# A decoder trunk on one core: the S5 input matrices are split and written ahead of the S5 preparation, and the first unit's products go by weight rows

## The chip, the cores and the metric

The kernel runs on 1 core of one Trainium2 chip. The metric is device time in microseconds (us) of one execution; the median of three is given. Times inside an execution are microseconds from the start of its span. The engines are TensorE (PE; its weight loads are PEld), VectorE (DVE), ScalarE (ACT), GpSimd (POOL) and SyncE (SP, which here only issues DMAs). ACT and POOL issue DMAs too.

## The reference, cut to what matters

One layer, 256 positions, 2048 channels, all float32. The normalised input is projected by one wide matrix; three branches of 1024 channels (gated MLP, S5, stick-breaking attention) are gated, projected and added; an MLP of 8192 follows.

```python
h = rmsnorm(x, norm1_g[l])
proj = h @ w_in[l]
...
bb_re = k_re[..., None] * b_re - k_im[..., None] * b_im
bu_re = jnp.einsum('blgh,gph->blgp', u, bb_re)
...
_, _, s_re, s_im = lax.associative_scan(combine, (a_re, a_im, bu_re, bu_im), axis=1)
y = (jnp.einsum('blgp,ghp->blgh', s_re, c_re.astype(f32))
     - jnp.einsum('blgp,ghp->blgh', s_im, c_im.astype(f32)))
...
g = jax.nn.gelu(y)
out = g * jax.nn.sigmoid(g @ w_glu.astype(f32) + b_glu.astype(f32))
```

The S5 input matrices are `b_re` and `b_im`. The attention masks its scores, takes a softplus, sums it along the keys by a triangular matmul and exponentiates; the masked form is what POOL computes below.

## The kernel before, in words

**Weights by units.** All weights are read once, in 512 KB units of 256 rows by 512 columns (or the same bytes in a wider form). For each unit SP loads `raw` (L195; 4 buffers), ACT rounds it to `hi` (L214) and DVE subtracts `lo = raw - hi`; every DVE operation has line 86, that of the helper which meters it. TensorE multiplies hi by the split activations' hi and lo, and lo by their hi: three products in the place of one float32 product. `whi` and `wlo` hold 4 units each; `begin_unit(u)` asks for the conversion of unit u+3, so ACT and DVE work some units ahead and ACT mostly waits until TensorE gives a `hi` buffer back.

**Order.** PE, DVE, ACT and SP run in the order in which the program writes their instructions (`MANUAL`). POOL is not in that list: the framework's scheduler sets POOL's order by its own estimate of when each instruction is ready, and every engine then waits in its order at run time. The plan of units is: s5 (units 0 to 15), q0 (16 to 23), k0 (24 to 31), v0 (32 to 39), q1 (40 to 47), k1, v1, the two halves of vg and u (to 95), gates and branches (to 223), and the S5 branch's GLU from unit 224.

**Side work by credit.** Everything beside the units is a generator in the list `tasks`: the norm's sums (`rows`), the S5 preparation (`s5p`), the split of the S5 input matrices (`s5b`), the splits of S5's input (`su0`, `su1`), the S5 recurrence (`s5`), attention (`att0`, `att1`). After each unit `pump()` adds 2560 ns less what DVE's instructions since the last pump cost by the rule in `Metered` (65 + 1.042 ns per element of a row, or 0.52 in three cheap forms; 180 in place of 65 up to 128 elements); the credit is capped at two units. It then goes through the list from the front; each task runs until it yields BAR (it wants the next unit) or the credit is used up. `spawn` puts a task in front, or behind all others with `front=False`.

**Around the change.** In unit 7 `s5p` and then `s5b` are put at the back. `s5b` (L511 to L525) loads `br` (512 KB, from ACT's queue, L515), waits two units, rounds it to `bh` on ACT (L520), subtracts `bl` on DVE, waits one more, and POOL writes both to DRAM (`bd`, L524 and L525); it does this for two halves. `s5p` has only small DVE operations, two Sin on ACT (L586, L587), and no BAR between L589 and its end. `s5_go` waits until `s5p`, `s5b`, `su0` and `su1` are gone and three units more, then `s5_run` starts: POOL reads `bd` and the split input `ud` back in blocks (`bs`, L658; `su`, L659), DVE builds the first table (`tt`, `cs`), TensorE multiplies (`pb`, L672), and so on for 16 chunks. `do_glu` (L1066) first drains whatever is left of `s5`, down to the split of its result `gs`.

The norm's row factors take the path: `r_s` on DVE, its power on POOL (`r_r`, L385), `diag` on DVE, `prow` on TensorE (L500), `rbc` on ACT (L502); each step one unit after the last. The result of the first s5 group is multiplied by `rbc` on DVE into `s5x`, which gives its PSUM banks back to q0's products (unit 16). In attention's first pair of heads, `pz` on TensorE (L845), `za` on ACT (L852), its mask on POOL (L854), Abs, Exp and Ln on ACT (`le`, L859 to L861), `sp` on DVE and `pc` on TensorE (L871) follow each other from unit 40 to unit 45.

Of the kernel before, what the change touches and what calls it, by code (L numbers as in the profile page):

```python
# [17 lines left out]
P = 128  # L18
# [73 lines left out]
def hybrid_trunk(  # L92
# [22 lines left out]
    V, S, G, PE = Metered(nc.vector), nc.scalar, nc.gpsimd, nc.tensor  # L115
# [14 lines left out]
    def a4(shape, dt, name):  # L130
        return acts.tile(shape, dt, tag="a4", name=name)
# [68 lines left out]
    def conv_to(n, parts=1):  # L200
        while nconv[0] <= min(n, len(units) - 1):
            u = nconv[0]
            dma_to(u)
            raw = raws[u]
            raws[u] = None
            if u >= len(units) - 4:
                hi, lo = (a4([P, 2, 512], F32R, f"{n_}{u}") for n_ in ("hi", "lo"))
            else:
                hi = whi.tile([P, 2, 512], F32R, tag="hi", name=f"hi{u}")
                lo = wlo.tile([P, 2, 512], F32R, tag="lo", name=f"lo{u}")  # L210
            w = 2 // parts
            for j in range(parts):
                k = slice(j * w, j * w + w)
                S.copy(hi[:, k, :], raw[:, k, :])  # L214
                V.tensor_sub(lo[:, k, :], raw[:, k, :], hi[:, k, :].bitcast(F32))
            loaded[u] = (hi, lo)
            nconv[0] += 1
# [26 lines left out]
    def spawn(name, gen, front=True):  # L244
        tasks.insert(0 if front else len(tasks), (name, gen))
# [5 lines left out]
    def flush():  # L251
        due = [f for n, f in late if n <= slot[0]]
        late[:] = [e for e in late if e[0] > slot[0]]
        for f in due:
            f()
# [4 lines left out]
    def begin_unit(u, lead):  # L260
        dma_to(u + 5)
        conv_to(u + lead)
        flush()
        return loaded.pop(u)

    def end_unit():
        pump()
        slot[0] += 1

    def two_banks(name):  # L270
        return ps_mm.tile([P, 2, 512], F32, tag="mm", name=name)
# [34 lines left out]
    def run_T(us, src, evac, lead=3, mid=None, delay=1):  # L306

        pt = two_banks(f"mm{us[0]}")
        ps = [pt[:, b, :].rearrange("p (e t) -> p e t", e=2) for b in range(2)]
        nk = len(us)  # L310
        for i, u in enumerate(us):
            hi, lo = begin_unit(u, lead)
            for nb in range(4):
                po = ps[nb // 2][:, nb % 2, :]
                for k in range(2):
                    kt = 2 * i + k
                    wh = hi[:, k, nb * P:(nb + 1) * P]
                    PE.matmul(po, lhsT=wh, rhs=src.hi(kt), start=kt == 0 and nb % 2 == 0, stop=False)  # L318
                    PE.matmul(po, lhsT=wh, rhs=src.lo(kt), start=False, stop=False)  # L319
                if nb == 1 and mid is not None:  # L320
                    mid(i)
            for nb in range(4):
                po = ps[nb // 2][:, nb % 2, :]
                for k in range(2):
                    kt = 2 * i + k
                    PE.matmul(po, lhsT=lo[:, k, nb * P:(nb + 1) * P], rhs=src.hi(kt), start=False,  # L326
                              stop=kt == 2 * nk - 1 and nb % 2 == 1)
            if i == nk - 1:
                for b in range(2):
                    late.append((slot[0] + delay, lambda b=b: evac(b, ps[b])))  # L330
                flush()
            end_unit()
# [96 lines left out]
    def load_x(c):  # L429
        S.dma_start(xt[c], x[:, c * 512:(c + 1) * 512].rearrange("(a p) c -> p a c", p=P))  # L430
# [49 lines left out]
    def x_half(i):  # L480
        c, half = divmod(i, 2)
        split_scaled([xf[c][:, 2 * half + j, :] for j in range(2)], xs, 2 * i, C_G1)

    def norm1_sums():
        for c in range(4):
            for tt in range(NT):
                sumsq(xt[c][:, tt, :], ss1[:, tt, c:c + 1], xt[c][:, tt, :])
            yield BAR
        yield from norm1_rows()
# [21 lines left out]
    def s5_split_b():  # L511

        for i in range(2):
            br = a4([P, 4, 2 * P], F32, f"br{i}")
            S.dma_start(br, s5_b[:, 4 * i:4 * i + 4])  # L515
            yield BAR
            yield BAR
            hi = a4([P, 4, 2 * P], F32R, f"bh{i}")
            lo = a4([P, 4, 2 * P], F32R, f"bl{i}")
            S.copy(hi, br)  # L520
            V.tensor_sub(lo, br, hi.bitcast(F32))
            yield 1135
            yield BAR
            G.dma_start(bd[:, 4 * i:4 * i + 4, 0, :], hi)  # L524
            G.dma_start(bd[:, 4 * i:4 * i + 4, 1, :], lo)  # L525

    def s5_split_u(i):
        hi = a4([P, 4, T], F32R, f"uh{i}")
        lo = a4([P, 4, T], F32R, f"ul{i}")
        S.copy(hi, s5x[i])  # L530
        V.tensor_sub(lo, s5x[i], hi.bitcast(F32))
        yield 1135
        yield BAR
        G.dma_start(ud[:, 4 * i:4 * i + 4, 0, :], hi)
        G.dma_start(ud[:, 4 * i:4 * i + 4, 1, :], lo)
# [431 lines left out]
    def do_proj(kind, i, us):  # L967
        dsts = {"s5": s5x, "q": qT, "k": kT, "u": uT}[kind]

        def ev(b, ps):  # L970
            if dsts[i] is None:
                dsts[i] = a4([P, 4, T], F32, f"{kind}{i}")
            dst = dsts[i]
            o = dst[:, 2 * b:2 * b + 2, :]
            V.tensor_mul(o, ps if kind == "s5" else wide_sum(ps, f"w{kind}{i}_{b}"), rb)
            if kind == "u":
                def act():
                    S.activation(o, o, AF.Gelu_apprx_tanh)
                    if i == 1 and b == 1:
                        gm["u"] = True  # L980

                later(1, act)
            if kind == "s5" and b == 1:
                spawn(f"su{i}", s5_split_u(i))
                if i == 1:
                    spawn("s5", s5_go(), front=False)

        if kind == "s5":
            run_T(us, xs, ev)
        else:  # L990
            for j, u in enumerate(us):
                run_W([(u, lambda ps, j=j: ev(j, ps))], xs)
# [57 lines left out]
    def do_branch(n, d, us):  # L1050
        if n != 1:
            drain({2: "att1", 0: "gmlp"}[n])

        def ev(tt, ps):
            if n == 2:
                merged[d] = gate[n, d]
            g = gate[n, d][:, tt, :]
            m = merged[d][:, tt, :]
            V.tensor_mul(g, g, ps)
            if n != 2:  # L1060
                V.tensor_add(m, m, g)
            if n == 1 and tt == 1:
                spawn(f"mt{d}", merged_T(d))

        run_N(us, {2: yc, 0: ya, 1: yb}[n], ev)
# [90 lines left out]
    for kind, arg, us in plan:  # L1156
        if kind == "s5" and arg == 0:
            x_half(0)
            conv_to(0, parts=2)

            def ev0(b, ps):
                V.tensor_mul(s5x[0][:, 2 * b:2 * b + 2, :], ps, rb)
                if b == 1:
                    spawn("su0", s5_split_u(0))

            def mid0(i):
                if i == 0:
                    x_half(1)
                elif i in (1, 3, 5):
                    x_half(i + 1)  # L1170
                    conv_to(i + 1)
                    x_half(i + 2)
                conv_to(max(i + 1, {4: 6, 5: 7, 6: 8, 7: 10}.get(i, 0)))
                if i in (2, 3, 4, 5):
                    load_x(i - 2)
                if i == 6:
                    spawn("rows", norm1_sums())
                if i == 7:
                    spawn("s5p", s5_prep(), front=False)
                    spawn("s5b", s5_split_b(), front=False)  # L1180

            run_T(us, xs, ev0, lead=0, mid=mid0, delay=8)
        elif kind in ("s5", "q", "k", "u"):
            do_proj(kind, arg, us)
        elif kind in ("v", "vg"):
            do_nat(kind, arg, us)
        elif kind.startswith("gate"):
            do_gate(int(kind[4]), arg, us)
        elif kind.startswith("br"):
            do_branch(int(kind[2]), arg, us)  # L1190
        elif kind == "glu":
            do_glu(arg, us)
        elif kind == "out":
            do_out(arg, us)
        elif kind == "m1":
            do_m1(*arg, us)
        else:
            do_m2(*arg, us)
# [74 lines left out]
```

## Time and profile before

| what | value |
|---|---|
| median of 3 runs | 1553.64 us (1553.34 to 1557.04) |
| profiled execution, its own time | 1557.89 us |
| its span, first to last instruction | 1556.2 us |
| granted TensorE clock, mean | 0.993 of full |
| busy: PE, DVE, ACT, POOL | 1532.5, 1097.4, 763.1, 67.6 us |

Busy time is the sum of an engine's instructions. "Idle before, and its releaser" in a timeline row says how long the engine stood before the instruction and what ended that. A view of waits sums the same by pair. A clock of 1.00 is 2.4 GHz, 0.50 is 1.2 GHz; in a stretch with both the mean stands.

### The profile page before, as it was taken

What the parts mean: (1) busy time and instruction counts of PE and PEld (TensorE: products, weight loads), DVE (VectorE), ACT (ScalarE), POOL (GpSimd) and SP (SyncE); (2) the same over time, 40 slices, a digit from 0 to 9 for tenths busy, and PEclk for the clock granted to TensorE, in tenths of its full rate; (3) what the DMA queues carried; (4) which work ended last, traced back from release to release, by engine and by line L of the source; (5) the groups of instructions that cost most, each with busy time, mean ns of one, the idle gap of its engine ahead of it and who ended that gap; (6) DMA issues with size and microseconds to landing.
All of it is one profiled execution on the core that took longest, in us unless ns stands there. A gap on an engine that the chain in (4) does not pass through costs nothing.

```text
span 1556.2 us, 20753 instructions
## 1 busy us (share of the span) xinstructions
PE 1532.5 (98%) x7900; PEld 1307.7 (84%) x7900; DVE 1097.4 (71%) x1454; ACT 763.1 (49%) x947; POOL 67.6 (4%) x126
## 2 busy tenths in 40 slices
PE   9998999999999999999999999999999999999997
PEld 9986888888888888888888888888888888888886
DVE  6894798999999999967655665556545655556554
ACT  7445658554555554555445443344443443344442
POOL 0101111000101100000000000000000000000000
PEclk9998999999999999999999999999999999999998
DMA  8866566666766766646665555555555555555653
GB/s 328 259 209 201 151 206 192 206 182 200 229 199 210 217 203 198 204 159 201 196 223 183 189 187 197 191 190 190 189 192 197 182 191 198 191 190 190 216 192 106
DMA packets 97411, 308.67 MB, mean 198 GB/s; under 512 B 11296, under 2 KB 22560, under 8 KB 97312
## 3 DMA queue, kind: packets, MB, share of 16 engines
q1 hardware_dynamic: 79200, 285.25, 56.0%
q0 software_dynamic: 11904, 10.49, 3.3%
q10 hardware_dynamic: 6208, 11.61, 2.3%
q8 instruction: 62, 1.02, 0.3%
q14 instruction: 37, 0.30, 0.1%
HBM read 301.02 MB, written 6.29 MB: 197 GB/s over the span
## 4 chain that ended last, share of the span: by engine, by line
PE 89%; issue 5%; DVE 2%; ACT 1%; DMA 1%; POOL 0%; SPq 0%; POOLq 0%; DVEq 0%; ACTq 0%
PE mm L349 19%; PE mm L350 19%; PE mm L352 19%; PE mm L289 18%; PE mm L293 9%; PE mm L319 1%; PE mm L318 1%; PE mm L326 1%; PE py L770 1%; DVE lo L86 1%; DMA bd<-bh 0%; ACT hi L214 0%; PE pb L672 0%; DMA raw<-in_w_in 0%; DMA raw<-in_w_m 0%
## 5 line engine op out<-in xcount | busy, mean ns | idle before, releaser
L86 DVE TENSOR_TENSOR lo<-raw,hi 128x1024 fp32r<-128x1024 f32 (+1 forms) x537 | 652.8, 1220 | 389.2 <-ACT hi L214 373.7
L214 ACT CAST hi<-raw 128x1024 fp32r<-128x1024 f32 (+1 forms) x537 | 561.4, 1049 | 623.5 <-PE mm L350 374.3
L289 PE MATMUL mm<-xz,hi 128*128 128x512 f32 x1024 | 256.5, 392 | 0.0
L289 PEld LDWEIGHTS mm<-xz,hi 128*128 128x128 f32 x1024 | 184.5, 189 | 33.0
L349 PE MATMUL mm<-hi,xs 128*128 128x512 f32 x512 | 200.9, 392 | 0.0
L350 PE MATMUL mm<-hi,xs 128*128 128x512 f32 x512 | 199.6, 390 | 0.0
L350 PE MATMUL mm<-hi,ff 128*128 128x512 f32 x480 | 186.9, 389 | 0.0
L349 PE MATMUL mm<-hi,ff 128*128 128x512 f32 x480 | 186.9, 389 | 0.0
L293 PEld LDWEIGHTS mm<-xz,lo 128*128 128x128 f32 x1024 | 139.8, 191 | 9.9
L293 PE MATMUL mm<-xz,lo 128*128 128x256 f32 x1024 | 142.8, 283 | 0.0
L352 PE MATMUL mm<-lo,xs 128*128 128x512 f32 x512 | 137.0, 390 | 0.0
L352 PE MATMUL mm<-lo,ff 128*128 128x512 f32 x480 | 128.3, 389 | 0.0
L349 PEld LDWEIGHTS mm<-hi,xs 128*128 128x128 f32 x512 | 96.2, 188 | 21.9 <-ACT bu L679 2.1
L352 PEld LDWEIGHTS mm<-lo,xs 128*128 128x128 f32 x512 | 96.2, 188 | 20.1
L350 PEld LDWEIGHTS mm<-hi,xs 128*128 128x128 f32 x512 | 96.3, 188 | 19.2
L352 PEld LDWEIGHTS mm<-lo,ff 128*128 128x128 f32 x480 | 90.1, 188 | 18.7
L349 PEld LDWEIGHTS mm<-hi,ff 128*128 128x128 f32 x480 | 90.1, 188 | 18.7
L350 PEld LDWEIGHTS mm<-hi,ff 128*128 128x128 f32 x480 | 90.2, 188 | 18.4
L289 PE MATMUL mm<-xs,hi 128*128 128x512 f32 x384 | 97.7, 397 | 0.0
L289 PEld LDWEIGHTS mm<-xs,hi 128*128 128x128 f32 x384 | 69.8, 191 | 12.6
L86 DVE TENSOR_TENSOR rt<-bu,cs 128x1024 f32<-128x1024 f32 x64 | 76.3, 1218 | 0.2
L293 PEld LDWEIGHTS mm<-xs,lo 128*128 128x128 f32 x384 | 52.4, 190 | 3.8
(252 smaller groups left out, 1689.3 us busy)
## 6 DMA issues: line engine op xcount, KB each, us to landing
raw<-in_w_m SPq DMA_DIRECT2D x256, 512.0 KB, 4.3
raw<-in_w_in SPq DMA_DIRECT2D x143, 512.0 KB, 4.2
raw<-in_w_wide SPq DMA_DIRECT2D x48, 512.0 KB, 4.2
raw<-in_w_br SPq DMA_DIRECT2D x48, 512.0 KB, 4.2
raw<-in_w_out SPq DMA_DIRECT2D x32, 512.0 KB, 4.0
x<-in_x ACTq DMA_DIRECT2D x8, 512.0 KB, 5.9
raw<-in_w_glu SPq DMA_DIRECT2D x8, 512.0 KB, 4.2
su<-ud POOLq DMA_DIRECT2D x48, 64.0 KB, 5.3
```

What stands on the lines that cost most here:

```text
L86: return fn(*a, **kw)
L214: S.copy(hi[:, k, :], raw[:, k, :])
L289: PE.matmul(pt[:, nb, :], lhsT=hi[:, k, nb * P:(nb + 1) * P], rhs=src.both(4 * i + k), start=4 * i + k == 0, stop=False)
L293: PE.matmul(pt[:, nb, T:], lhsT=lo[:, k, nb * P:(nb + 1) * P], rhs=src.hi(4 * i + k), start=False, stop=4 * i + k == last)
L318: PE.matmul(po, lhsT=wh, rhs=src.hi(kt), start=kt == 0 and nb % 2 == 0, stop=False)
L319: PE.matmul(po, lhsT=wh, rhs=src.lo(kt), start=False, stop=False)
L326: PE.matmul(po, lhsT=lo[:, k, nb * P:(nb + 1) * P], rhs=src.hi(kt), start=False, stop=kt == 2 * nk - 1 and nb % 2 == 1)
L349: PE.matmul(ps[tt], lhsT=xh, rhs=hi[:, k, :], start=kt == 0, stop=False)
L350: PE.matmul(ps[tt], lhsT=xl, rhs=hi[:, k, :], start=False, stop=False)
L352: PE.matmul(ps[tt], lhsT=xh, rhs=lo[:, k, :], start=False, stop=kt == 2 * nk - 1)
L770: PE.matmul(py[h][32 * i:32 * i + 32, :T], lhsT=cks[h][:, ri, i, :], rhs=s[i // 2][:, ri, i % 2, :], start=ri == 0, stop=ri == 1, tile_pos ...
```

## The change

Two edits. In unit 7 `s5b` is put into the list ahead of `s5p` in place of behind it; nothing in the two tasks differs. In `run_T`, for unit 0 alone, the first 16 products go through the four column blocks with the first half of the weight rows (k = 0) and then through them with the second, in place of both halves for each block; the loop is written flat for all units, and `mid` is called after the same number of products.

```diff
@@ run_T
-            for nb in range(4):
+            order = [(nb, k) for nb in range(4) for k in range(2)]
+            if u == 0:
+                order.sort(key=lambda e: e[1])
+            for n, (nb, k) in enumerate(order):
                 po = ps[nb // 2][:, nb % 2, :]
-                for k in range(2):
-                    kt = 2 * i + k
-                    wh = hi[:, k, nb * P:(nb + 1) * P]
-                    PE.matmul(po, lhsT=wh, rhs=src.hi(kt), start=kt == 0 and nb % 2 == 0, stop=False)
-                    PE.matmul(po, lhsT=wh, rhs=src.lo(kt), start=False, stop=False)
-                if nb == 1 and mid is not None:
+                kt = 2 * i + k
+                wh = hi[:, k, nb * P:(nb + 1) * P]
+                PE.matmul(po, lhsT=wh, rhs=src.hi(kt), start=kt == 0 and nb % 2 == 0, stop=False)
+                PE.matmul(po, lhsT=wh, rhs=src.lo(kt), start=False, stop=False)
+                if n == 3 and mid is not None:
                     mid(i)
@@ mid0
                 if i == 7:
+                    spawn("s5b", s5_split_b(), front=False)
                     spawn("s5p", s5_prep(), front=False)
-                    spawn("s5b", s5_split_b(), front=False)
```

## Rows read from the trace of the kernel before

**Rows 1.** The page: busy time of each engine, share of the span, instructions

```profile
PE 1532.5 (98%) x7900; PEld 1307.7 (84%) x7900; DVE 1097.4 (71%) x1454; ACT 763.1 (49%) x947; POOL 67.6 (4%) x126
```

**Rows 2.** Waits of PE, whole span: for whom, us in total, times, longest

```profile
PE pc L871 <- DVE sp L86: 7.6, 1, 7.6
PE mm L318 <- ACT gs L398: 1.6, 1, 1.6
PE mm L318 <- ACT hi L214: 1.5, 1, 1.5
PE pyc L888 <- ACT le L880: 0.5, 1, 0.5
```

**Rows 3.** Timeline of POOL around 120 us: start, us, instruction, idle before

```profile
119.19 0.78 POOL L524 DMA_DIRECT2D bd<-bh  x1 [53.93 <-ACT bh L520]
120.82 0.75 POOL L525 DMA_DIRECT2D bd<-bl  x1 [0.85 <-DVE bl L86]
126.68 1.07 POOL L658 DMA_DIRECT2D bs<-bd  x2 [5.11 <-DMA bd<-bh]
...
132.87 0.42 POOL L854 TENSOR_SCALAR_AFFINE_SELECT za<-za 128x256 f32<-128x256 f32 x1
```

**Rows 4.** Timeline of ACT, 124 to 140 us

```profile
124.60 0.49 ACT L852 ACTIVATE za<-pz 128x384 f32<-128x384 f32 x1 [0.16 <-PE pz L846]
...
126.45 1.05 ACT L214 CAST hi<-raw 128x1024 fp32r<-128x1024 f32 x1 [1.36 <-PE mm L289]
134.23 0.84 ACT L859 ACTIVATE le<-za 128x768 f32<-128x768 f32 x1 [6.73 <-POOL za L854]
...
138.54 0.84 ACT L861 ACTIVATE le<-le 128x768 f32<-128x768 f32 x1
```

**Rows 5.** Timeline of DVE: the second split, and the first S5 table

```profile
141.49 1.22 DVE L86 TENSOR_TENSOR bl<-br,bh 128x1024 fp32r<-128x1024 f32 x1
...
154.80 1.43 DVE L86 TENSOR_TENSOR tt<-e,e 128x256 f32<-128x256 f32 x4
156.26 0.76 DVE L86 TENSOR_TENSOR cs<-tt,tt 128x256 f32<-128x256 f32 x2
```

**Rows 6.** Stretches: length, PE, PEld, DVE, ACT, POOL busy, PEclk, DMA share, GB/s

```profile
5.00:10.00 5.00, 3.54 (x31) 3.34 (x30) 2.43 (x6) 2.73 (x5) 0.00 (x0) 1.00 0.98 364
...
146.10:153.29 7.19, 7.19 (x29) 6.26 (x30) 4.23 (x5) 2.73 (x3) 0.00 (x0) 0.63 0.96 294
176.41:180.97 4.56, 4.56 (x30) 4.11 (x29) 4.53 (x7) 0.30 (x1) 0.00 (x0) 1.00 0.45 97
674.95:682.90 7.95, 7.60 (x48) 7.41 (x49) 6.23 (x8) 6.19 (x8) 0.00 (x0) 0.79 0.30 87
682.90:688.66 5.76, 5.76 (x50) 5.76 (x49) 2.45 (x2) 1.86 (x3) 0.00 (x0) 1.00 0.53 186
```

**Rows 7.** DMA issues of 0 to 200 us: KB each, median us to landing

```profile
br<-in_s_b ACTq DMA_DIRECT2D x2, 512.0 KB, 7.2
```

**Rows 8.** Timelines of POOL, DVE and PE: the norm's row factors and s5's first evacuation

```profile
40.43 0.70 POOL L385 TENSOR_TENSOR r_r<-r_s,mhalf 128x2 f32<-128x2 f32 x1 [38.72 <-DVE emag_p L86]
...
43.09 0.48 DVE L86 TENSOR_SCALAR diag<-ident,r_r 128x128 f32<-128x128 f32 x2
...
44.67 0.61 PE L500 MATMUL prow<-diag,ones 128*128 128x128 f32 x4
...
51.19 1.23 DVE L86 TENSOR_TENSOR lo<-raw,hi 128x1024 fp32r<-128x1024 f32 x1 [1.60 <-ACT hi L214]
52.34 1.28 DVE L86 TENSOR_TENSOR s5x<-mm,rbc 128x512 f32<-128x512 f32 x2
...
53.76 2.09 PE L289 MATMUL mm<-xs,hi 128*128 128x512 f32 x8
```

**Rows 9.** Timelines of ACT and PEld: the second unit's cast and its first weight load

```profile
8.86 1.05 ACT L214 CAST hi<-raw 128x1024 fp32r<-128x1024 f32 x1 [0.51 <-DMA raw<-in_w_in]
...
10.00 0.19 PEld L318 LDWEIGHTS mm<-xs,hi 128*128 128x128 f32 x1
```

## The prediction

> **What bounds the kernel now.** I read the page first: TensorE is busy 98% of the span [rows 1], so only what makes it stand, or run at a lower clock, can be won. The waits of TensorE come next [rows 2]: one of 7.6 us (`pc` of attention's first heads, for `sp` on DVE), one of 1.6 us before the GLU (for S5's `gs`), one of 1.5 us in unit 0, one of 0.5 us. Then I followed the 7.6 us back through three timelines. POOL has the mask `za` behind reads of `bd`, and a read waits until the write of `bd` has landed: the write of the high half is issued at 119.19, its reads at 126.68, and the mask runs only at 132.87, 12.05 us after the low half's write at 120.82 [rows 3], although ACT had the second `za` ready at 124.60 + 0.49 = 125.1 [rows 4]. Behind the mask, Abs, Exp and Ln hold ACT's order from 134.23 to 139.4, 5.15 us with two table loads [rows 4]; the casts, the splits and `sp` follow, and `pc` starts at 146.10. TensorE had been free since 146.10 - 7.6 = 138.5. Last, the stretches give the clock after each stand: from `pc` through one unit takes 7.19 us at a mean 0.63, the same work one pair of heads later 4.56 us at 1.00 [rows 6]. The stand thus costs 7.6 + 2.6 = 10.2 us.
>
> **The change part by part.**
>
> *The split goes first, so the mask is free: +10.2.* I worked the credit through by the kernel's own rule. For the order before it puts the start of `s5_run` at unit 47, where DVE's table stands (154.80 [rows 5]), and `y` of the last heads' S5 product after unit 223. For the changed order: the first load after unit 7, its casts after unit 9, its writes after unit 11, the second half's at 11, 13 and 18; `s5p` ends after unit 40 (39 before, since two splits at 1132 ns of credit go ahead of it) and `s5_run` starts at 43. All writes of `bd` and the first reads lie then some 60 us before the mask, which can run at 125.1 + 0.4, before ACT is through its next cast at 126.45 + 1.05 = 127.5 [rows 4]. The reads of the third chunk wait for TensorE alone and come later in the program. The old stand goes, with its clock.
>
> *What is late next: -1.9, and -1.9 of clock.* Ln ends at 127.5 + 5.15 = 132.65. From Ln's end to `pc` it took 146.10 - 139.4 = 6.7 us; of the links in that, the second half's split (1.22) is gone, but the table of the first chunk, which now falls to unit 43, stands in DVE's order ahead of `sp`: 1.43 + 0.76 = 2.2 [rows 5]. So `pc` starts at 132.65 + 6.7 - 1.2 + 2.2 = 140.4, and TensorE waits 140.4 - 138.5 = 1.9. Bounds: 0 (the table one unit later, behind `sp`) and 3.1 (the split's 1.2 ran beside ACT's casts and its absence saves nothing). Whether the clock falls after so short a stand: after the 1.5 us of unit 0 the clock was 1.00, after the GLU's 1.6 us and one more short wait two units took 7.95 us at 0.79 in place of 5.76 at 1.00 [rows 2, 6]. Bounds 0 and 2.2 - 0.3 = 1.9; I take 1.9, as 1.9 us of standing is nearest to the GLU's 1.6 + 0.3.
>
> *The heads' next wait: -0.4.* One `pyc` waits 0.5 us today [rows 2]; with S5 already running a like wait may appear for the first heads. Bounds 0 and 0.8.
>
> *S5 ends earlier: +3.8.* Starting four units sooner, it ends less far ahead, as credit that is lost at the cap today (5120 at unit 47) is not there to lose: by the same arithmetic the last rotation ends after unit 220 (221 before), `y` after 222, its evacuation after 223, and only the split of `gs` is left to drain, which runs beside unit 223's products. That removes 1.6 us of wait and 7.95 - 5.76 = 2.2 of short wait and low clock [rows 2, 6]. Bounds: 0 and 3.8.
>
> *Two new near misses: -0.3 each.* The planner leaves two units, 5.76 us [rows 6], between a load of `br` and its cast, and the load took 7.2 [rows 7]; ACT, and DVE behind it, would stand 1.4 us twice. The first time DVE is about to reduce the norm's sums: `diag` ends at 43.57, `prow` comes at 44.67, so 1.1 us are covered and 0.3 reach TensorE [rows 8]. The second time DVE must free s5's banks: it had 1.60 us of idle ahead of 51.19, and the evacuation ends at 53.62 against unit 16's start at 53.76 [rows 8]; 1.4 just fits. I take 0.3 for each, bounds 0 and 1. The raw loads that SP issues behind DVE's `lo` slip by the same 1.4 us; they run four buffers ahead, and TensorE's `hi` three units. If that cover were gone, each would cost its lateness one for one. POOL's writes of `bd` (0.78 + 0.75 [rows 3]) fall among `r_r` and the writes of `ud`; `su` is split one to four units later and nobody waits, as `s5_go` waits for `s5p` anyway.
>
> By the Trainium skill, page "DMA: Bandwidth & Descriptors", section "Anatomy of one DMA", a POOL-issued DMA takes about 2.0 us plus its bytes over 436 GB/s, 3.2 us for 512 KB as an estimate. The rows do not agree (7.2 us for a load, 7.5 from write to read); by that figure both near misses would be nothing, the sum 9.8, and the first rival below would lose its price.
>
> *Unit 0: 0.* The order lets 8 products run before the second half's cast, so six fewer come after. But unit 1's cast ends at 8.86 + 1.05 = 9.91, bound by a DMA, and PE loads its first weights at 10.00 [rows 9]. At most 0.1 us.
>
> **Sum.** 10.2 - 1.9 - 1.9 - 0.4 + 3.8 - 0.6 = 9.2 us off the profiled execution's 1557.9. That one lies 4.3 us above the median; no stand above is peculiar to it, so I take the same off the median: 1553.6 - 9.2 = 1544.4.
>
> **The rivals.**
>
> *A: reads of the high half stand ahead of the norm's power on POOL.* POOL's order is the scheduler's. Before, it put reads ahead of a mask that became ready about 6 us after the write [rows 3, 4]; `r_r` would be ready about 2.9 us (one unit) after it, which speaks for `r_r` first, but not by much. If not: the write is issued at 40.43 - 2.88 + 1.4 = 39.0, the reads wait 7.5 and take 1.07, then 0.70 and 0.48: `prow` at 48.8 in place of 44.67, 4.1 + 2.6 of clock [rows 3, 6, 8], less the 0.3 counted. Gain 2.8: 1550.8. Chance 0.15.
>
> *B, slower than before: reads of the low half too.* Its write follows at 40.6, the read holds POOL 12.05 us from there, so `r_r` starts at 52.65 and `prow` at 53.8: 9.2 + 2.6 - 0.3 = 11.5 lost against 9.2, so 1555.9. It decides once `r_r` starts later than 40.43 + 1.1 + 6.9 = 48.4. Against it: the low half is ready for reading 1.6 us after the high half. Chance 0.07.
>
> *C: the GLU's stand stays*, if the evacuation slips a unit (the last rotation has one unit to spare): 1544.4 + 3.8 = 1548.2. Chance 0.17.
>
> *D: the change doesn't free the mask*, POOL placing other reads before it: the gain is 3.8 - 0.6 = 3.2, so 1550.4. Only the chunk-3 reads could do it. Chance 0.10.
>
> **How the numbers follow.** The forecast has 0.51. With every bound in favour the gain is 14.0, so 1539.6; the cases A, C and D reach to 1551. Left out: B and tails, under 2 in 10. A measurement of this kernel tells some 0.3%, 4.7 us, from no change, so "faster" is below 1549.0: nearly all of the forecast (0.48), two thirds of C (0.12), a third of A and D (0.09): 0.69; slower, above 1558.3, 0.05 from B and its tail; the rest is the same.
>
> **What would show it.** Right: `bd` written before 60 us; the mask within 1 us of `za` near 125; a PE wait for `sp` of 1 to 3 us in place of 7.6; the stretch after it at a clock above 0.63; no PE wait for `gs`; the table at unit 43, ahead of `sp`. Wrong: a PE wait at `prow` or at unit 16 above 1 us (A, B, or a slow `br`), a `gs` wait (C), a mask behind a read (D). The forecast fails if credit does not place the table and the last rotation where I worked them out, or if the short stand keeps its clock (then 1.9 better).

## The result, and the profile after

The changed kernel takes 1546.09 us (median; 1545.78 to 1547.07), the kernel before in the same set 1555.34 us (1553.34 to 1558.5): ratio 0.994, 95% interval 0.9919 to 0.996. The profiled execution after took 1545.78 us with a span of 1544.1 us, 12.1 us shorter than before.

The page: TensorE is still the bound, and busy 4.1 us less than in [rows 1].

```profile
PE 1528.4 (99%) x7900; PEld 1303.8 (84%) x7900; DVE 1097.1 (71%) x1454; ACT 764.0 (49%) x947; POOL 67.3 (4%) x126
```

Waits of PE after, the counterpart of [rows 2] (lines have moved down by two):

```profile
PE pc L873 <- DVE sp L86: 1.7, 1, 1.7
PE mm L320 <- ACT hi L214: 1.3, 2, 0.6
PE pwarm L467 <- POOL ones L452: 1.0, 1, 1.0
PE mm L289 <- DVE s5x L86: 0.3, 1, 0.3
```

A stand, here and below, is a time in which TensorE waits. The 7.6 us have become 1.7, the waits for `gs` and at `pyc` are gone, and a short one for `s5x` is new. The third line is PE's wait for its very first operand, and it is 1.0 us in every kernel of this document, the one before included.

POOL's timeline after, 37 to 126 us, against [rows 3]:

```profile
37.29 0.95 POOL L526 DMA_DIRECT2D bd<-bh  x1 [35.57 <-ACT bh L522]
39.37 0.75 POOL L527 DMA_DIRECT2D bd<-bl  x1 [1.12 <-DVE bl L86]
40.55 0.72 POOL L387 TENSOR_TENSOR r_r<-r_s,mhalf 128x2 f32<-128x2 f32 x1 [0.43 <-DVE s_a L86]
49.50 1.11 POOL L660 DMA_DIRECT2D bs<-bd  x2 [8.23 <-DMA bd<-bh]
52.25 2.11 POOL L660 DMA_DIRECT2D bs<-bd  x4 [1.64 <-DMA bd<-bl]
...
125.25 0.41 POOL L856 TENSOR_SCALAR_AFFINE_SELECT za<-za 128x256 f32<-128x256 f32 x1 [48.29 <-ACT za L854]
```

The read of `bd` still holds POOL, for 8.23 us, but at 41 us, where nobody waits for POOL; `r_r` went ahead of it. The mask starts at 125.25, 0.1 us after `za` (next fence: 124.68 + 0.49).

ACT's and DVE's timelines after, against [rows 4, 5]:

```profile
124.68 0.49 ACT L854 ACTIVATE za<-pz 128x384 f32<-128x384 f32 x1 [0.56 <-PE pz L848]
...
127.19 1.05 ACT L214 CAST hi<-raw 128x1024 fp32r<-128x1024 f32 x1 [1.36 <-PE mm L289]
128.14 0.84 ACT L861 ACTIVATE le<-za 128x768 f32<-128x768 f32 x1
...
132.45 0.84 ACT L863 ACTIVATE le<-le 128x768 f32<-128x768 f32 x1
```

```profile
134.27 1.23 DVE L86 TENSOR_TENSOR lo<-raw,hi 128x1024 fp32r<-128x1024 f32 x1 [4.77 <-ACT hi L214]
135.41 1.42 DVE L86 TENSOR_TENSOR tt<-e,e 128x256 f32<-128x256 f32 x4
136.87 0.76 DVE L86 TENSOR_TENSOR cs<-tt,tt 128x256 f32<-128x256 f32 x2
137.54 1.22 DVE L86 TENSOR_TENSOR lo<-raw,hi 128x1024 fp32r<-128x1024 f32 x1
...
140.00 0.95 DVE L86 SCALAR_TENSOR_TENSOR sp<-za,le 128x768 f32<-128x768 f32 x1
```

Abs now follows its cast without idle time, 6.1 us earlier (128.14 against 134.23). DVE then has the first S5 table (`tt`, `cs`), which stood at 154.80 before, between Ln and `sp`.

PE's timeline at `pc`, and the stretches after, against [rows 6]:

```profile
141.01 0.70 PE L873 MATMUL pc<-sp,ntri 128*128 128x256 f32 x2 [1.73 <-DVE sp L86]
```

```profile
141.01:148.93 7.92, 7.92 (x49) 7.16 (x50) 5.19 (x9) 2.64 (x4) 3.18 (x6) 1.00 0.63 181
...
665.03:670.79 5.76, 5.76 (x50) 5.76 (x49) 5.17 (x7) 5.10 (x7) 0.00 (x0) 1.00 0.38 140
```

Both stretches run at a clock of 1.00, where [rows 6] had 0.63 and 0.79. Before, `pc` to the first `pyc` took 9.98 us; now 7.92, with one group of `pb` products (0.57) more in it, so 2.63 us of clock came back there. In the GLU's first two units it is 7.95 - 5.76 = 2.19, of which 7.95 - 7.60 = 0.35 was the short wait for `gs` and the rest clock [rows 6].

**Where the 12.1 us came from.** The same instructions stand at these times in the two traces:

| landmark on TensorE | before | after | gained since the last |
|---|---|---|---|
| unit 16's first product | 53.76 | 54.52 | -0.76 |
| first `pz` | 123.09 | 123.83 | 0.02 |
| first `pc` | 146.10 | 141.01 | 5.83 |
| first `pyc` | 156.08 | 148.93 | 2.06 |
| GLU's first `gs` product | 674.95 | 665.03 | 2.77 |
| end | 1556.2 | 1544.1 | 2.18 |

The 5.83 are 7.56 - 1.73 of stand. 2.06 + 0.57 are the clock after it. The 2.77 hold 1.6 of `gs` wait, 0.5 of `pyc` wait (the second heads', at 187 us before) and the 0.57 again, as the `pb` products done early are not left for later. The 2.18 are the short wait and the clock after the `gs` stand, 0.35 and 1.8. The 0.76 lost at the start are taken up with the near misses below.

### The profile page after: what moved, and what is told of

Same layout as the page of the kernel before. It is cut to its first block, busy times and chain, and to the rows that moved or that the text cites. A ratio compares the mean times of both kernels' runs of the same rounds, so it can differ in the third digit from the quotient of the medians.

```text
span 1544.1 us, 20755 instructions
## 1 busy us (share of the span) xinstructions
PE 1528.4 (99%) x7900; PEld 1303.8 (84%) x7900; DVE 1097.1 (71%) x1454; ACT 764.0 (49%) x947; POOL 67.3 (4%) x126
## 4 chain that ended last, share of the span: by engine, by line
PE 96%; DVE 1%; issue 1%; ACT 1%; DMA 1%; SPq 0%; POOLq 0%; POOL 0%; DVEq 0%; ACTq 0%
PE mm L289 21%; PE mm L351 19%; PE mm L352 19%; PE mm L354 19%; PE mm L293 11%; PE mm L320 1%; PE mm L321 1%; PE mm L328 1%; PE py L772 1%; PE pb L674 0%; DMA raw<-in_w_in 0%; ACT hi L214 0%; DVE lo L86 0%; DMA raw<-in_w_m 0%; DVE x L86 0%
```

## The experiments

Ratios are to the kernel before, timed in the same set; spans and waits are of the profiled execution.

**1. The swap alone.** Unit 0 keeps its old order.

```diff
                 if i == 7:
-                    spawn("s5p", s5_prep(), front=False)
                     spawn("s5b", s5_split_b(), front=False)
+                    spawn("s5p", s5_prep(), front=False)
```

> The kernel before with s5b ahead of s5p and nothing else. Theory (all of the gain is the freed mask and the earlier end of S5; unit 0's order gives nothing, because unit 1's cast ends it): the profile again shows a PE wait for sp of 1.7 us, none for gs, the clock at 1.00 in both places, and a time within 1 us of the full change, some 9 us below the kernel before. Rival (the order of unit 0 carries a part): 0.7 us or more above the full change, with unit 1 starting later by as much.

Measured: 1545.95 us (1545.48 to 1547.45), ratio 0.9937 (0.992 to 0.9953), the full change's time within its spread. PE waits 1.7 at `pc`, 1.5 for `s5x`, and not for `gs`. So the swap makes the whole difference.

**2. The order of unit 0 alone.** The first hunk of the change, put into the kernel before.

> The kernel before with unit 0's products by weight rows and nothing else. Theory: eight products run ahead of the second half's cast, but the second unit's products start where its cast ends, so the 1.5 us wait of unit 0 splits into two of about 0.6 us each and the time is that of the kernel before within 0.5 us; the wait for sp of 7.6 us and that for gs stay. Rival: 0.7 us faster, six products' time.

Measured: 1554.69 us (10 runs, 1551.15 to 1558.57) against 1556.5 (20 runs, 1551.41 to 1558.18), ratio 0.9995 (0.9982 to 1.0007): no difference. The waits of PE, of which two lines suffice:

```profile
PE pc L873 <- DVE sp L86: 7.6, 1, 7.6
...
PE mm L320 <- ACT hi L214: 0.2, 1, 0.2
```

The wait for `hi` falls from 1.5 [rows 2] to 0.2 (in the full change it is 1.3, in two parts, as was expected here). But unit 1 starts at 9.75 here, bound by its own cast, and at 10.11 before; that little doesn't show in the time, and in the full change, with the same order, unit 1 starts at 10.28.

**3. The split left late, the first reads of `bd` moved off POOL.** The kernel before, with the reads of the first two chunks issued from ACT's queue (as float32 on both sides).

```diff
-                G.dma_start(bs[rows], bdv[...])
+                if ch < 2:
+                    S.dma_start(bs[rows].bitcast(F32), bdv[...].bitcast(F32))
+                else:
+                    G.dma_start(bs[rows], bdv[...])
```

> The kernel before, the s5b task still behind s5p, but the first two chunks' reads of bd are issued from ACT's queue in program order, so that nothing stands ahead of the mask on POOL. Theory (the reads in POOL's order were the stall): the mask runs within 1 us of za, Ln ends 7 us earlier, the PE wait for sp falls from 7.6 to 0.8 us (split of the second half still ahead of sp), the stretch behind it keeps a higher clock, the gs wait stays: 6 to 10 us below the kernel before. Rival (it is the split's own work, its casts, DVE time and DMA, beside attention that stalls TensorE): the wait for sp stays above 5 us and the time within 3 us.

Measured: 1547.81 us (1546.65 to 1548.53), ratio 0.9949 (0.9934 to 0.9964). POOL's timeline and the waits of PE:

```profile
119.27 0.78 POOL L524 DMA_DIRECT2D bd<-bh  x1 [53.91 <-ACT bh L520]
120.90 0.75 POOL L525 DMA_DIRECT2D bd<-bl  x1 [0.85 <-DVE bl L86]
124.59 0.41 POOL L857 TENSOR_SCALAR_AFFINE_SELECT za<-za 128x256 f32<-128x256 f32 x1 [2.94 <-ACT za L855]
```

```profile
PE mm L318 <- ACT gs L398: 1.6, 1, 1.6
...
PE pc L874 <- DVE sp L86: 0.7, 1, 0.7
PE pyc L891 <- ACT le L883: 0.7, 1, 0.7
```

The writes are as late as before, yet the mask waits for `za` alone and `pc` for 0.7 us. ACT issues the reads at 143.75 and 148.33, when the writes have long landed, so they hold nothing there either. The stand came from the reads in POOL's order. The `gs` wait is untouched, as S5 starts no earlier. The table is at 147.83, behind `sp`.

**4. One half of the split early.** The changed kernel with `s5b` as two tasks, one half ahead of `s5p` and one behind; `s5_split_b` takes the half as its argument (not shown). In the first kernel half 0 goes early, as below, in the second half 1.

```diff
-                    spawn("s5b", s5_split_b(), front=False)
+                    spawn("s5b0", s5_split_b(0), front=False)
                     spawn("s5p", s5_prep(), front=False)
+                    spawn("s5b", s5_split_b(1), front=False)
```

> The full change with only the first half of the split put ahead of s5p; the second half is split behind s5p, around units 40 and 41, beside attention. Theory: the mask is free as in the full change; by the credit's arithmetic s5_run starts at unit 44 in place of 43, so the table stands behind sp and the new wait of 1.7 us goes; the last rotation still ends after unit 220, so no gs wait; unit 16 no longer waits for the evacuation (0.35 us). So 1 to 2.5 us below the full change. Rival (the second half's work beside attention costs TensorE): a wait for sp of over 2 us.

Measured with half 0 early: 1544.95 us (1544.68 to 1545.88), ratio 0.9932 (0.9918 to 0.9947). `pc` waits no more; the waits of PE and DVE's timeline:

```profile
PE pyc L890 <- ACT le L882: 1.6, 1, 1.6
```

```profile
136.66 0.95 DVE L86 SCALAR_TENSOR_TENSOR sp<-za,le 128x768 f32<-128x768 f32 x1
138.52 1.42 DVE L86 TENSOR_TENSOR tt<-e,e 128x256 f32<-128x256 f32 x4
139.98 0.76 DVE L86 TENSOR_TENSOR cs<-tt,tt 128x256 f32<-128x256 f32 x2
```

The table has slipped behind `sp` but stands ahead of the subtraction that feeds the heads' last exponential, so the wait moved on to `pyc` and, against the expectation, didn't go away. The full change took 1.1 us more, with ranges that just touch; in the profiles that is mostly its early stands for `hi` and `s5x` (1.3 + 0.3), 0.2 here. The stand for `hi` falls in the first 11 us, where the two programs don't differ, so it goes with the execution, and how much of the 1.1 us is the edit's these runs don't tell.

> The mirror of the last one: the second half early, the first half, which the first chunks read, split behind s5p at units 40 and 41. POOL's order here has the mask ahead of the reads (the write comes one unit later than in the kernel before). Theory (order on POOL alone decides): PE wait for sp under 1 us although the first half's casts, splits, writes and reads all lie beside attention; time as the half-0 variant within 2 us, unless the first product of S5 waits for its reads. Rival (the work beside attention stalls it): a wait over 4 us.

Measured with half 1 early: 1545.33 us (two runs, 1545.23 and 1545.43), ratio 0.9934 (0.9914 to 0.9954); PE waits 1.6 at `pyc`, nothing at `pc`. POOL's timeline:

```profile
122.95 0.78 POOL L526 DMA_DIRECT2D bd<-bh  x1 [57.81 <-ACT bh L522]
124.21 0.75 POOL L527 DMA_DIRECT2D bd<-bl  x1 [0.49 <-DVE bl L86]
124.97 0.78 POOL L856 TENSOR_SCALAR_AFFINE_SELECT za<-za 128x256 f32<-128x256 f32 x2
128.27 1.09 POOL L660 DMA_DIRECT2D bs<-bd  x2 [2.53 <-DMA bd<-bh]
```

The half that the first reads need is written here 3.8 us later than before the change, beside the mask, and neither the mask nor `pc` waits for it: the scheduler has placed the reads behind the mask. So writing early isn't what is needed; the place of the reads in POOL's order decides. Early writing is one way to put them elsewhere.

**5. The recurrence one unit earlier.** The changed kernel with two units of pause in `s5_go`.

```diff
-        for _ in range(3):
+        for _ in range(2):
             yield BAR
```

> The full change with s5_go waiting two units in place of three, so that S5's first table is issued in unit 42 in place of 43. Theory (the new 1.7 us wait is the table standing ahead of sp in DVE's order): the table runs in DVE's idle time before the cast that follows Ln, sp comes 2.2 us sooner, the PE wait for sp falls from 1.7 to under 0.3 us and none appears at pyc (unlike the half-0 variant, where the table came behind sp and held the next step instead); 1.5 to 2 us below the full change. Rival (sp is late by the attention chain itself): the wait stays above 1 us.

Measured: 1544.48 us (1544.19 to 1544.95), ratio 0.9928 (0.9912 to 0.9944). The waits of PE and DVE's timeline:

```profile
PE pc L873 <- DVE sp L86: 0.2, 1, 0.2
```

```profile
129.49 1.43 DVE L86 TENSOR_TENSOR tt<-e,e 128x256 f32<-128x256 f32 x4
130.95 0.76 DVE L86 TENSOR_TENSOR cs<-tt,tt 128x256 f32<-128x256 f32 x2
```

The table runs while DVE stands idle for Ln, and the wait falls from 1.7 to 0.2: the table was the new wait. (For `s5x` PE waits 1.0 here, where nothing differs from the full change up to there and it waited 0.3: that wait goes with the execution.)

**6. Both: half 0 early, and one unit of pause.** The hunk of experiment 4, and

```diff
-        for _ in range(3):
-            yield BAR
+        yield BAR
         yield from s5_run()
```

> The half-0 variant with one unit of waiting in s5_go, which puts the table into unit 42 there too. Theory: no PE wait for sp, for pyc, for s5's evacuation at unit 16 or for gs; what remains are the waits of the first 10 us. 1.5 us below the half-0 variant, 2 to 3.5 us below the full change, so some 1543. Rival: the second half's split, now close before the table on DVE, makes sp late again: a wait of 1 us or more.

Measured: 1543.25 us (6 runs, 1542.78 to 1543.93), ratio 0.992 (0.9907 to 0.9933), the best of all: 2.8 us under the full change, and the two ranges, though of different sets, don't touch. Of the 2.7 us between the two profiled spans 1.1 is the wait for `hi`, which goes with the execution. Beside the 1.0 us for its first operand PE waits 0.2 at `pc` and 0.2 for `hi`; the table stands at 128.24, before Ln is through.

**7. The recurrence as late as before.** The changed kernel with seven units of pause, so that S5 starts at unit 47 again, the split still early.

```diff
-        for _ in range(3):
+        for _ in range(7):
             yield BAR
```

> The changed kernel with the S5 recurrence held back four units more, so that it starts at unit 47 as it did in the kernel before; the split and the writes of the input matrices stay early. What is open: was the end of S5 earlier only because its start was (then the stand for gs before the GLU comes back with its low clock, some 2 to 3.8 us), or because two splits of credit had been spent earlier (then it stays away). Theory, start decides: PE waits for gs 1.6 and 0.3 as before, a clock below 1.00 in the two units after it; the first table goes behind sp, so the wait at pc shrinks from 1.7 to below 1, and a pyc wait of some 0.5 returns. Sum against the changed kernel: +3.8 - 1.2 + 0.5 = some 3 us, so 1547.8 to 1550. Rival, credit decides: no gs wait, time 1544 to 1546.

Measured: 1548.03 us (1547.69 to 1548.44), ratio 0.9946 (0.9929 to 0.9963). The waits of PE and the stretches of 5 us from 660 on:

```profile
PE mm L320 <- ACT gs L400: 1.6, 1, 1.6
...
PE pyc L890 <- ACT le L882: 0.5, 1, 0.5
...
PE mm L321 <- DVE gs L86: 0.3, 1, 0.3
```

```profile
660.00:665.00 5.00, 3.97 (x30) 2.53 (x28) 2.15 (x3) 2.17 (x4) 0.00 (x0) 1.00 0.90 288
665.00:670.00 5.00, 4.13 (x23) 3.93 (x24) 4.48 (x7) 4.16 (x7) 0.00 (x0) 0.76 0.07 27
670.00:675.00 5.00, 5.00 (x40) 5.00 (x39) 3.01 (x3) 3.38 (x4) 0.00 (x0) 0.90 0.66 208
```

The `gs` stand is back with its low clock, and so is the `pyc` wait; the one at `pc` is gone. So it is the earlier start of S5, not the credit spent early on the split, that freed the GLU. With the split early and S5 late, `pc` waits for nothing at all.

**8. The split one unit earlier still.** `s5b` put into the list in unit 6, to bring about the first rival: reads of `bd` ahead of `r_r` on POOL.

```diff
                     spawn("rows", norm1_sums())
-                if i == 7:
                     spawn("s5b", s5_split_b(), front=False)
+                if i == 7:
                     spawn("s5p", s5_prep(), front=False)
```

> The full change with s5b put into the list in unit 6 in place of 7. POOL's order then has three reads of bd ahead of the norm's power. Theory (a read that waits for its write holds everything behind it on POOL; the forecast's rival A made real): the power starts some 3 us late or more, diag and prow after it, TensorE waits at prow 2 to 5 us, with up to 2.6 us of clock, so 2 to 7 us above the full change, while the mask near 125 stays free. Rival (the reads land in time, as they are short): no wait at prow, time as the full change.

Measured: 1550.21 us (1548.41 to 1550.66), ratio 0.996 (0.9944 to 0.9976), 4.1 us over the full change. POOL's and PE's timelines, and the stretches after the second stand:

```profile
37.04 0.95 POOL L526 DMA_DIRECT2D bd<-bh  x1 [35.33 <-ACT bh L522]
...
43.62 1.60 POOL L660 DMA_DIRECT2D bs<-bd  x3 [4.56 <-DMA bd<-bh]
45.24 0.75 POOL L387 TENSOR_TENSOR r_r<-r_s,mhalf 128x2 f32<-128x2 f32 x1
```

```profile
46.36 0.71 PE L502 MATMUL prow<-diag,ones 128*128 128x128 f32 x4 [1.51 <-DVE diag L86]
57.83 3.25 PE L289 MATMUL mm<-xs,hi 128*128 128x512 f32 x8 [2.13 <-DVE s5x L86]
```

```profile
54.00:60.00 6.00, 3.87 (x21) 3.27 (x20) 5.79 (x13) 1.05 (x1) 0.00 (x0) 0.87 1.08 348
60.00:66.00 6.00, 6.00 (x32) 5.27 (x31) 2.95 (x4) 3.66 (x4) 1.49 (x2) 0.85 0.43 131
```

Rival A is real, one unit away: the reads stand ahead of `r_r`, `prow` waits 1.5 us (2 to 5 were expected), and DVE, which stood with it, is then late for `s5x` (2.1 us). The clock stays at 1.00 after the first stand and falls after the second: at 0.87 and 0.85 twelve microseconds lose 6 x 0.13 + 6 x 0.15 = 1.7. The three sum to 5.3; less the 0.3 that `s5x` waits in the full change, 5.0, against 4.8 between the two spans. When the kernel ran, the write was issued only 0.25 us earlier than in the full change (37.04 against 37.29), since ACT was busy right up to its cast (35.70). What the one unit flipped is the order that the scheduler had fixed beforehand.

## Why the prediction was right, and where its terms were off

The likeliest case came, with 1546.09 inside the range and faster by over 0.3%. By the medians of its own set the gain is 1555.34 - 1546.09 = 9.25 us, against 9.2 predicted. That closeness is luck: in the profiled executions, on which the sum was made, the gain is 12.1. With the terms as measured the sum is 10.2 - 1.7 + 0 + 0.5 + 3.8 - 0.8 = 12.0. So the working was 2.8 short, 1.9 of it in the clock term and 0.9 at `pyc`. The medians hide that, because the kernel before has a median 2.55 us below its profiled execution (1557.89).

- **The old stand goes, 10.2: right.** The mask is freed (0.1 us behind `za`), the last of the writes is issued before 56 us, and the reads do not touch the mask. Experiment 3 shows the cause by itself: with the writes as late as before and only the reads off POOL's order, the stand falls to 0.7 us.
- **The new wait at `pc`, -1.9: right**, 1.73. The working holds by its links: Ln's end to `pc` took 141.01 - 133.29 = 7.72 us, and 6.7 - 1.2 + 2.2 = 7.7 was reckoned. Experiments 5 and 7 take the table away from there, in one direction each, and the wait falls to 0.2 and to nothing.
- **The clock after it, -1.9: mis-sized, it was 0.** This is the step that was off: "1.9 us of standing is nearest to the GLU's 1.6 + 0.3". The stand had the length reckoned, and the clock was 1.00 behind it. The prediction named this way of being wrong ("then 1.9 better"). The lower bound of 0 should have been given more weight, since [rows 2] and [rows 6] already held a stand of 1.5 us with no fall behind it.
- **The `pyc` wait, -0.4: mis-sized**, it was 0, and the 0.5 of before went too, a gain of 0.5. The wait that was feared is shown to exist by experiment 4 (1.6 us at `pyc`, once the table is behind `sp`): the table costs at one of the two places, not at both.
- **S5 ends earlier, +3.8: right.** `py` comes a unit earlier, `gs` is ready before the GLU wants it. Experiment 7 undoes the earlier start alone and gets the whole stand back.
- **The near misses, -0.3 each: the size about right, the reason not.** The load of `br` was issued earlier in its unit than reckoned, and its casts (35.93 and 46.85) didn't wait. At `prow` nothing stood. (In the profile of experiment 7 the first cast did wait for its load, 0.43 us.) At unit 16 PE waited 0.35 us, because the second split (`bl` at 48.23) and the `lo`s around it filled DVE, which left no idle time ahead of the evacuation (53.09, against 52.34 in [rows 8]). In three more executions with the same split it was 1.5, 1.0 and 0.4 (experiments 1, 5 and 7), once beyond the bound of 1: the term should have been reckoned from DVE's fill, not from the load. Of the rest of the 0.76 us by unit 16, 0.27 was lost by `prow` (44.94 against 44.67), 0.17 of that by unit 1's first product (10.28 against 10.11); 0.14 is not traced. By the Trainium skill, page "DMA: Bandwidth & Descriptors", section "Anatomy of one DMA", the estimate for a POOL-issued 512 KB is 3.2 us. The trace doesn't agree: `bd`'s writes of the high half land 8.9 us after their issue here (median of two), those of the low half 10.3. The prediction also held that figure against the near misses, but it is one for DMAs that POOL issues, and their load of `br` is issued by ACT.
- **Unit 0, 0: right.** Experiment 2's interval holds 1.
- **The base: a step that was not seen as one.** "I take the same off the median" took 9.2 from a median of three, 1553.64, where the sum had been made on an execution of 1557.89. Over 20 runs the kernel before has 1556.5 (1551.41 to 1558.18), and its clock, the mean over the span, goes with it on the whole: 0.997 in the fastest of them, 1552.87 to 1554.81 in the five at 0.996, 1557.55 to 1558.18 in the four at 0.993. A fall by 0.004 over 1550 us is 6.2 us, about the whole spread. The clock that a stand costs differs from execution to execution: in the profile of experiment 2, with the same 7.6 us stand, `pc` to `pyc` took 155.04 - 145.89 = 9.15 us, not 9.98. The changed kernel, whose stands left the clock at 1.00 in its profile, varies by 1.3 us over 4 runs. The prediction carried the clock terms of one execution as constants. Its base was 4.3 us under the profiled execution and its gain 2.9 under the measured 12.1. The two partly offset each other: the forecast of 1544.4 lies 1.4 us below the profiled execution after, 1.7 below its median.

**The rivals.** A did not come (`r_r` went first) but stands one unit away; its price was put at 6.4 us in all and measured 4.1. Its wait at `prow` was 1.5, not 4.1, as the write landed sooner (43.62 - 37.04 = 6.6 us to the read, where 7.5 was taken, from an issue 2 us earlier than the 39.0 assumed; in the full change, too, it came at 37.29), and the rest came back at `s5x` and in the clock after it. B, the slower one, did not come: in neither kernel did a low half's read stand ahead of `r_r`. (Its time, 1555.9, lies below the 1558.3 above which the prediction called a result slower, so the 0.05 that it was given there was too much.) C came only when S5's start was put back by hand; the time there, 1548.03, is near the 1548.2 that C was given, but with no wait at `pc` in it. D did not come.

## What to carry to other kernels

On POOL here, a DMA that waited for another DMA's landing held the compute queued behind it: before an optimisation of the producer, look at which instruction stands behind the waiting read and whether the read can be issued from another queue or later. Where a scheduler fixes an engine's order by its own estimates, a shift by one unit can flip it, so trace the order again after every move. And when a long stand goes, find the link that moves into the gap: here a 2.2 us table which cost 1.7 us at one place, 1.6 at the next, and 0.2 when it was started in idle time.

## What the runs showed of the hardware that was not expected

**Like stands, unlike clocks.** Stands of 1.73 us (`pc`, full change), 1.57 us (`pyc`, experiment 4), 1.51 us (`s5x`, experiment 1) and 1.51 us (`prow`, experiment 8) left the granted clock at 1.00; 1.56 us before `gs` and 0.34 behind it were followed by a stretch of 5 us at 0.66 to 0.76 in all four traces that had them (before, and experiments 2, 3 and 7), and 2.13 us at `s5x` by 0.87 and 0.85. Length alone doesn't order these: 1.73 us kept the clock and 1.56 + 0.34 didn't, and at `s5x` 1.51 kept it and 2.13 didn't. What the engine did ahead of them differs (the GLU's stand follows `py`, products with 32 columns of weights), but whether that decides it no run here settles.

**The same write, very unlike landings.** From the issue of `bd`'s high half to the first read behind it, a read that POOL's queue held until the landing in all three, it took 49.50 - 37.29 = 12.2 us in the full change, 43.62 - 37.04 = 6.6 in experiment 8, and 128.27 - 122.95 = 5.3 in experiment 4. What stretches it wasn't tried; a plan that hangs on one such figure, as rival A's price did, needs the range.
